# A recurrent block's gates computed gate by gate, and three output products that read their activations ahead, into the place of their low parts

## The chip, the cores and the metric

The kernel runs on one core of one Trainium2 chip, as one program. The metric is the device time of one execution in microseconds. The core has a matrix engine (TensorE, PE in the profile), a vector engine (VectorE, DVE), a scalar engine (ScalarE, ACT), a general engine (GpSimd, POOL) and a sync engine (SyncE, SP), which here only issues DMAs. Each engine works through its own instructions in order and waits on semaphores for the others.

## What is computed

One inference step of a model of two layers on 512 prompt rows and 8 x 16 sample rows (640 tokens, five tiles of 128). The first layer is recurrent, the second is stick-breaking attention with 16 heads. Between the two, the residual stream is normed and projected to shared keys and values. What the change touches, cut from the reference:

```python
def rg_lru(x, h0, w_r, b_r, w_i, b_i, lam):
    r = jax.nn.sigmoid(block_diag(x, w_r, b_r))
    i = jax.nn.sigmoid(block_diag(x, w_i, b_i))
    log_a = -LRU_C * r * jax.nn.softplus(-lam)
    a = jnp.exp(log_a)
    u = jnp.sqrt(-jnp.expm1(2.0 * log_a)) * (i * x)
    ...                                   # h = a * h + u along time

def recurrent_mixer(hn, ...):
    xb, zg = jnp.split(hn @ w_in, 2, axis=-1)
    xb, conv_new = causal_conv(xb, conv0, conv_w, conv_b)
    y, hT = rg_lru(xb, h0, ...)
    return (y * jax.nn.silu(zg)) @ w_out, hT, conv_new

x = x + gate * rms_norm(out, g_post[l])   # after each layer
```

The model's width D is 2048, the recurrent width 4096. Everything is fp32.

## The kernel before

**Precision.** A product of two fp32 operands is made of three matmuls of rounded operands: high by high, high by low, low by high (`mm3`, lines 101 to 103). A high part is a copy on ACT that rounds (`wh` line 87, `yh` line 777), the low part is the difference on DVE (`wl` line 88, `yl` line 778). Every weight and every activation tile that comes from memory therefore passes through ACT and then DVE before PE can use it. The split weights have three places (`WB`), their raw form four (`RB`, tag `wr`).

**The recurrent stage** (`recurrent`) goes through 16 blocks of 256 recurrent features, two halves of 128. For a block, `silu_gates` and `conv` make two products with the input weight `w_in` (`pair_product`): a scheme with seven instead of eight block products, over four accumulators in PSUM called `pc`, `pa`, `pb`, `pd`. The seven units have the names S1, X11, S4, S2, X12, S3, X22; each is 21 matmuls of 128x320. Two plain products with `xv` stand between S4 and S2. `keep` (line 561) copies an accumulator to SBUF on ACT so that its bank can be used again: `pa` holds X11, then S2, then S3, and each of these has to be copied before the next begins. The weights are split some steps ahead by a generator that `ahead` moves on, at a high priority (`urgent`).

`lru` computes the two gates r and i of the block: for each half and each gate two column halves, each a group of six matmuls in one of four banks (`psg`), and a sigmoid on ACT (line 702). Then come, in a fixed chain, Exp and Tanh on ACT (lines 712 and 716, with a table load), some operations on DVE, Sqrt (line 724, another table load), the scan along time, and the store of the block's y to DRAM (`yd`).

**The output products** (`out_product`) run three times: over the first 16 K tiles of the recurrent output, over the second 16, and over the attention's output (`yd` twice, then `od`). A product goes through chunks of one 512 column block and some token tiles; in its first chunk it also loads its 16 activation tiles, two ahead of their use, each into a raw tile `yr` that takes one of the four places of `wr`, and splits it into `yh` and `yl`. Those live in a ring of 8 tiles of four K tiles each (tag `h`), which the normed activations use too.

**Beside the second of them**, `mid` adds the residual to the finished token tiles: `residual` (line 851) reads x in four pieces a token tile into `xx`, two of which exist. The last head of the attention runs in one stretch with the beginning of the third product.

**What sets the order.** The instructions of an engine are put in order when the kernel is built, by a scheduler that follows the order of the program, readiness and priorities (`high_priority`). A tile's place is waited for by the first instruction that writes into it; a DMA that waits holds the queue of its issuing engine, SP for the weights, activations and x.

Of the kernel before, what the change touches and what calls it, by code (L numbers as in the profile page):

```python
# [11 lines left out]
F32 = mybir.dt.float32  # L12
# [36 lines left out]
class Trunk:  # L49
# [487 lines left out]
    def pair_product(self, ep, evac):  # L537


        nc = self.nc  # L540
        kw = dict(skip_group_check=True)

        def bank(n):
            return self.ring("quad", 4, n)[:, :HALF]

        def seven(ps, i, first):
            hi, lo = self.weights()
            c = slice(HALF * i, HALF * i + HALF)
            for n, x in enumerate(self.pairs):
                self.mm3(ps, hi[:, n, :], lo[:, n, :], x[:, 0, c], x[:, 1, c], first and n == 0, n == NP - 1, **kw)  # L550
            self.ahead()

        def plain(ps, w, half, first):
            c = slice(HALF * half, HALF * half + HALF)
            for n, k in enumerate(PLAIN):
                mh, ml = self.hT[k]
                self.mm3(ps, w[0][:, n, :], w[1][:, n, :], mh[:, c], ml[:, c], first and n == 0, k == KD - 1, **kw)

        def keep(ps, tag="keep", bufs=2):
            t = ep.tile([P, HALF], F32, tag=tag, name=tag, bufs=bufs)  # L560
            nc.scalar.activation(t, ps, AF.Copy)
# [24 lines left out]
        evac(1, 1, a, p5, ALU.add)  # L586
        seven(d, X22, False)
        evac(0, 1, d, u3, ALU.subtract)
# [94 lines left out]
    def lru(self, j, ep, block, zs):  # L683
        nc = self.nc
        V, A, G = nc.vector, nc.scalar, nc.gpsimd
        pv2, st, xf, xh, xl = block
        gw = [self.weights() for _ in range(2)]
        gate_bank = lambda n: self.half(n, "psg2") if n < 2 else self.bank("psg2")
        rs, qs = [], []
        for h in range(2):  # L690
            pv = pv2[:, h, :]
            fs = slice(P * h, P * h + P)
            g = []
            for i in range(2):
                hi, lo = gw[i]
                v = ep.tile([P, T], F32, tag="gq"[i], name="gq"[i], bufs=2)
                for c in range(2):
                    ps = gate_bank((2 * i + c) % 4)[:, :HALF]
                    s = slice(HALF * c, HALF * c + HALF)
                    for k in range(2):  # L700
                        self.mm3(ps, hi[:, k, fs], lo[:, k, fs], xh[k][:, s], xl[k][:, s], k == 0, k == 1)
                    last = A.activation(v[:, s], ps, AF.Sigmoid, bias=pv[:, 5 + i : 6 + i])
                g.append(v)
            rs.append(g[0])
            V.tensor_tensor(xf[h], g[1], xf[h], ALU.mult)
        self.ahead()


        for h in range(2):
            q = ep.tile([P, T], F32, tag="q", name="q", bufs=2)  # L710
            with self.tc.issue_after(last.ins):
                last = A.activation(q, rs[h], AF.Exp, scale=self.nk8[:, 2 * j + h : 2 * j + h + 1])
            qs.append(q)
        for h in range(2):
            with self.tc.issue_after(last.ins):
                last = A.activation(rs[h], rs[h], AF.Tanh, scale=self.k4[:, 2 * j + h : 2 * j + h + 1])
        for r, q in zip(rs, qs):
            e = ep.tile([P, self.HW + 1], F32, tag="tmp", name="e", bufs=self.TMP)[:, :T]
            V.tensor_scalar_add(q, q, 1.0)
            V.scalar_tensor_tensor(e, r, 1.0, q, op0=ALU.add, op1=ALU.mult)  # L720
            V.scalar_tensor_tensor(q, e, -4.0, q, op0=ALU.add, op1=ALU.mult)
        for r in rs:
            with self.tc.issue_after(last.ins):
                A.activation(r, r, AF.Sqrt, scale=0.25)
        for h, (r, q) in enumerate(zip(rs, qs)):
            f = 2 * j + h
            pv = pv2[:, h, :]
            V.scalar_tensor_tensor(r, r, -1.0, q, op0=ALU.mult, op1=ALU.mult)
# [12 lines left out]
        G.dma_start(self.O["state"][:, 2 * j : 2 * j + 2, :], st)  # L741
# [19 lines left out]
    def out_product(self, src, w, chunks, evac, fill=iter(())):  # L761


        nc = self.nc
        ys, slots = [], []

        def load(k):
            nonlocal slots
            if k % 4 == 0:
                slots = [self.hp.tile([P, 4, T], F32R, tag="h", name=n) for n in ("yh", "yl")]  # L770
            yh, yl = (x[:, k % 4, :] for x in slots)
            if k in self.local:
                raw = self.local[k]
            else:
                raw = self.wp.tile([P, self.WW], F32, tag="wr", name="yr", bufs=self.RB)[:, :T]
                nc.sync.dma_start(raw, src[P * k : P * k + P, :])
            self.last_split = nc.scalar.activation(yh, raw, AF.Copy).ins  # L777
            nc.vector.tensor_tensor(yl, raw, yh.bitcast(F32), ALU.subtract)  # L778
            ys.append((yh, yl))

        for c, (toks, n) in enumerate(chunks):
            cs = slice(512 * n, 512 * n + 512)
            ps = {t: self.acc("acc") for t in toks}

            def mm(k, t, hi, lo):
                ts = slice(P * t, P * t + P)
                yh, yl = ys[k]
                self.mm3(ps[t], yh[:, ts], yl[:, ts], hi, lo, k == 0, k == 15)

            last = c + 1 == len(chunks)  # L790
            early = 10 if last else 16
            for k in range(0, early, 2):
                hi, lo = self.wsplit(w[n, :, k : k + 2, :], 512)
                if len(ys) < 16:
                    load(k)
                    load(k + 1)
                for kk in range(2):
                    for t in toks:
                        mm(k + kk, t, hi[:, kk, :], lo[:, kk, :])
                if c > 0:  # L800
                    next(fill, 0)
# [84 lines left out]
    def attention_begin(self):  # L886
# [8 lines left out]
        return self.out_product(self.od, self.I["w_out_b"], chunks, gate)  # L895

    def attention_out(self, product):
        nc, O = self.nc, self.O
# [10 lines left out]
    def mid(self, oacc, ss, ss1, bp):  # L909
# [566 lines left out]
```

## Time and profile before

| | us |
|---|---|
| median of 3 runs | 2911.41 (2906.17 to 2912.74) |
| profiled execution | 2916.01 |
| its span | 2914.3 |
| recurrent stage | to about 1040 |
| product of the first 16 K tiles | 1046 to 1268 |
| product of the second 16, with the residual | to about 1550 |
| shared keys and values, heads, third product | to the end |

Times in the profile are microseconds from the span's start. A row of the timeline has the start, the duration, the engine, the line, the operation, output and inputs by their names in the program, shapes, a count, and in brackets the idle time before it with what ended it. Matmuls are pipelined: one lasts longer than the distance to the next, and that distance is the pace. In a window of PE, the columns are its length, busy time and matmuls, the granted clock of TensorE as a share of full speed, the DMA engines' mean share and their rate. A row of the view of waits gives who waited, for whom, the sum, how many times and the longest.

### The profile page before, as it was taken

How to read it: one execution, taken by the hardware profiler on the slowest of the kernel's cores; microseconds unless marked ns; L12 is line 12 of the kernel's file. 1: busy time of each engine (PE TensorE's matmuls, PEld its weight loads, DVE VectorE, ACT ScalarE, POOL GpSimd, SP SyncE). 2: the span in 40 equal slices, each digit the busy share in tenths (PEclk: the TensorE clock that was granted, in tenths of full speed). 3: DMA queues.
4: the chain of work that ended last, by engine and by line, in shares of the span. 5: the costliest groups of instructions: out<-in, count | busy, mean ns of one | idle time of the engine just before them, and what ended most of it. 6: DMA issues, size and time to landing. Idle time of an engine off the chain costs nothing.

```text
span 2914.3 us, 48223 instructions
## 1 busy us (share of the span) xinstructions
PE 2837.1 (97%) x18784; PEld 2520.8 (86%) x18784; DVE 1977.9 (68%) x2867; ACT 1607.8 (55%) x2464; POOL 420.3 (14%) x589
## 2 busy tenths in 40 slices
PE   6899999999999999999999999999999999999998
PEld 4799999999999977778788999778989999897886
DVE  7677776777677766634568877777666766667335
ACT  5466555655565566533456666674455555546323
POOL 0011222222222200001113322001000000001000
PEclk9899999999999999999999999999999999999999
DMA  9866676667666666555567666663565555656636
GB/s 338 303 143 150 162 163 152 146 164 160 158 146 162 143 195 190 167 147 163 186 209 254 226 209 214 203 200 115 185 197 168 182 175 183 198 169 197 208 109 224
DMA packets 246003, 536.49 MB, mean 184 GB/s; under 512 B 22520, under 2 KB 106616, under 8 KB 244624
## 3 DMA queue, kind: packets, MB, share of 16 engines
q1 hardware_dynamic: 219056, 442.01, 47.7%
q0 software_dynamic: 26720, 91.42, 15.5%
q8 instruction: 147, 2.41, 0.3%
q14 instruction: 80, 0.66, 0.1%
HBM read 496.24 MB, written 37.11 MB: 183 GB/s over the span
## 4 chain that ended last, share of the span: by engine, by line
PE 79%; ACT 6%; DVE 4%; DMA 2%; issue 2%; POOL 0%; DVEq 0%; POOLq 0%; SPq 0%; ACTq 0%
PE acc L101 7%; PE acc L102 7%; PE acc L103 7%; PE psh L101 6%; PE acck L101 5%; PE psh L103 5%; PE psh L102 5%; PE acck L103 5%; PE acck L102 5%; PE pa L101 3%; PE pa L103 3%; PE pa L102 3%; PE psa L198 2%; DVE wl L88 1%; PE pc L101 1%
## 5 line engine op out<-in xcount | busy, mean ns | idle before, releaser
L88 DVE TENSOR_TENSOR wl<-wr,wh 128x1024 fp32r<-128x1024 f32 x216 | 270.3, 1252 | 289.4 <-ACT wh L87 288.1
L87 ACT ACTIVATE wh<-wr 128x1024 fp32r<-128x1024 f32 x216 | 228.2, 1056 | 382.1 <-PE acc L103 228.6
L101 PE MATMUL acc<-wh,yh 128*128 128x512 f32 x960 | 378.8, 395 | 10.3 <-ACT yh L777 5.6
L102 PE MATMUL acc<-wl,yh 128*128 128x512 f32 x960 | 378.3, 395 | 7.7 <-DVE wl L88 7.7
L103 PE MATMUL acc<-wh,yl 128*128 128x512 f32 x960 | 377.0, 394 | 0.3 <-DVE yl L778 0.3
L186 DVE TENSOR_TENSOR wa<-wa,wa 128x1024 bf16<-128x1024 f32 (+1 forms) x256 | 308.6, 1240 | 24.9 <-ACT wa L185 22.7
L101 PE MATMUL psh<-nh,wh 128*128 128x320 f32 x1024 | 323.9, 316 | 0.0
L103 PE MATMUL psh<-nh,wl 128*128 128x320 f32 x1024 | 318.9, 311 | 0.0
L102 PE MATMUL psh<-nl,wh 128*128 128x320 f32 x1024 | 317.4, 310 | 0.0
L185 ACT ACTIVATE wa<-wa 128x1024 bf16<-128x1024 f32 x256 | 263.1, 1052 | 67.2 <-DVE wa L186 46.7
L101 PEld LDWEIGHTS acc<-wh,yh 128*128 128x128 f32 x960 | 182.1, 190 | 58.4 <-issue 8.7
L102 PEld LDWEIGHTS acc<-wl,yh 128*128 128x128 f32 x960 | 182.5, 190 | 47.7 <-DVE wl L88 10.3
L103 PEld LDWEIGHTS acc<-wh,yl 128*128 128x128 f32 x960 | 182.2, 190 | 39.9 <-DVE yl L778 2.2
L101 PEld LDWEIGHTS psh<-nh,wh 128*128 128x128 f32 x1024 | 192.3, 188 | 19.3 <-DVE ql L1112 12.6
L101 PE MATMUL pa<-xs,wh 128*128 128x320 f32 x630 | 194.8, 309 | 0.0
L103 PE MATMUL pa<-xs,wl 128*128 128x320 f32 x630 | 194.7, 309 | 0.0
L102 PE MATMUL pa<-xs,wh 128*128 128x320 f32 x630 | 194.7, 309 | 0.0
L103 PEld LDWEIGHTS psh<-nh,wl 128*128 128x128 f32 x1024 | 192.4, 188 | 0.5 <-DVE wl L88 0.2
L102 PEld LDWEIGHTS psh<-nl,wh 128*128 128x128 f32 x1024 | 192.4, 188 | 0.1
L101 PE MATMUL acck<-nh,wh 128*128 128x320 f32 x512 | 161.5, 315 | 0.0
L481 POOL DMA_DIRECT2D sum<-w_in_a_dram x90 | 79.4, 882 | 559.3 <-DVE wl L88 262.9
L103 PE MATMUL acck<-nh,wl 128*128 128x320 f32 x512 | 158.3, 309 | 0.0
(354 smaller groups left out, 7312.4 us busy)
## 6 DMA issues: line engine op xcount, KB each, us to landing
wa<-w_ada_dram SPq DMA_DIRECT2D x192, 512.0 KB, 4.7
wr<-w_out_a_dram SPq DMA_DIRECT2D x96, 512.0 KB, 4.1
sum<-w_in_a_dram POOLq DMA_DIRECT2D x90, 448.0 KB, 5.6
wr<-w_in_b_dram SPq DMA_DIRECT2D x64, 512.0 KB, 5.3
ck<-cache_k_dram SPq DMA_DIRECT2D x64, 512.0 KB, 6.7
cv<-cache_v_dram SPq DMA_DIRECT2D x64, 512.0 KB, 5.3
wr<-w_out_b_dram SPq DMA_DIRECT2D x56, 512.0 KB, 4.2
raw<-w_in_a_dram SPq DMA_DIRECT2D x60, 448.0 KB, 4.2
```

The costliest lines, as they stand in the source:

```text
L87: nc.scalar.activation(hi[:, :n], raw, AF.Copy)
L88: nc.vector.tensor_tensor(lo[:, :n], raw, hi[:, :n].bitcast(F32), ALU.subtract)
L101: mm(out, sh, mh, start=start, stop=False, **kw)
L102: mm(out, sh, ml, start=False, stop=False, **kw)
L103: mm(out, sl, mh, start=False, stop=stop, **kw)
L185: nc.scalar.activation(parts[i], raw, AF.Copy)
L186: nc.vector.tensor_tensor(parts[2] if i else raw, raw, parts[i], ALU.subtract)
L198: nc.tensor.matmul(ps[32 * j : 32 * j + 32, :], self.c3[:, 4 * g + j, :], ws[j // 2][i][:, j % 2, :], start=g + i == 0, stop=g == 3 and i ...
L481: self.nc.gpsimd.dma_start(self.big[tag], self.quarter(w, i), accum_op=ALU.add)
```

## The change

There are four edits. `keep` gets the high priority that the weights' splits have. `lru` computes the first gate for both halves, then the second gate for both, and moves the weights on after each gate. `out_product` reads an activation tile straight into the place of its low part, which DVE then overwrites; it reads groups of four K tiles, the first group before its first chunk, each next group when it begins to split the one before; the splits of the first four have a high priority. The last head's output, which never leaves the core, is named by `kept`. `mid` has six places for `xx` instead of two.

```diff
         def keep(ps, tag="keep", bufs=2):
             t = ep.tile([P, HALF], F32, tag=tag, name=tag, bufs=bufs)
-            nc.scalar.activation(t, ps, AF.Copy)
+            with self.tc.high_priority(200):
+                nc.scalar.activation(t, ps, AF.Copy)
             return t
...
-        for h in range(2):
-            pv = pv2[:, h, :]
-            fs = slice(P * h, P * h + P)
-            g = []
-            for i in range(2):
-                hi, lo = gw[i]
+        for i in range(2):
+            hi, lo = gw[i]
+            for h in range(2):
...
-                    ps = gate_bank((2 * i + c) % 4)[:, :HALF]
+                    ps = gate_bank(2 * h + c)[:, :HALF]
...
-        self.ahead()
+            self.ahead(1 - i)
...
+        def fetch(k):
+            hi, lo = (self.hp.tile([P, 4, T], F32R, tag="h", name=n) for n in ("yh", "yl"))
+            for kk in range(k, k + 4):
+                yh, yl = hi[:, kk - k, :], lo[:, kk - k, :]
+                if kk not in kept:
+                    nc.sync.dma_start(yl.bitcast(F32), src[P * kk : P * kk + P, :])
+                raws.append((yh, yl))
         def load(k):
-            if k in self.local:
-                raw = self.local[k]
-            else:
-                raw = self.wp.tile([P, self.WW], F32, tag="wr", name="yr", bufs=self.RB)[:, :T]
-                nc.sync.dma_start(raw, src[P * k : P * k + P, :])
-            self.last_split = nc.scalar.activation(yh, raw, AF.Copy).ins
-            nc.vector.tensor_tensor(yl, raw, yh.bitcast(F32), ALU.subtract)
+            if k % 4 == 0 and len(raws) < 16:
+                fetch(len(raws))
+            yh, yl = raws[k]
+            raw = self.local[k] if k in kept else yl.bitcast(F32)
+            with self.tc.high_priority(200 if k < 4 else 0):
+                self.last_split = nc.scalar.activation(yh, raw, AF.Copy).ins
+                nc.vector.tensor_tensor(yl, raw, yh.bitcast(F32), ALU.subtract)
             ys.append((yh, yl))
+        fetch(0)
...
-            ch = self.residual(t, oacc, ss, self.I["x"][ts, :], bp, 2)
+            ch = self.residual(t, oacc, ss, self.I["x"][ts, :], bp, 6)
```

**ACT in a recurrent block.** From Exp (`q<-g`) to the third copy of an accumulator, before:

```order
L712 ACTIVATE q<-g,nk_100 128x640
L716 ACTIVATE g<-g,k_99 128x640 x2
L561 ACTIVATE keep_3691<-pc_3663 128x320
L87 ACTIVATE wh<-sum_3182 128x896
L724 ACT_TABLE_LOAD
L724 ACTIVATE g<-g 128x640 x2
L87 ACTIVATE wh<-raw 128x896
L730 ACTIVATE q<-q,mone 128x640
L87 ACTIVATE wh<-rest 128x896
L730 ACTIVATE q<-q,mone 128x640
L561 ACTIVATE keep<-pa_3664 128x320
```

and with the change, the same stretch:

```order
L714 ACTIVATE q<-g,nk_100 128x640
L718 ACTIVATE g<-g,k_99 128x640 x2
L87 ACTIVATE wh<-sum_3182 128x896
L562 ACTIVATE keep<-pa_3664 128x320
L726 ACT_TABLE_LOAD
L726 ACTIVATE g<-g 128x640
L87 ACTIVATE wh<-raw 128x896
L726 ACTIVATE g<-g 128x640
L87 ACTIVATE wh<-rest 128x896
L732 ACTIVATE q<-q,mone 128x640
```

The copy of `pa` has moved from behind the table load, the Sqrts and two splits to ahead of them, and one Sqrt has fallen behind the split of `raw`.

**PE in the same block.** The last plain product (`pd` with `xv`) and what follows it, with buffer numbers, before:

```order
L102 MATMUL pd7_3749<-xv_1429,wh_3686 128x320
L103 MATMUL pd7_3749<-xv_1429,wl_3687 128x320
L101 MATMUL pb7_3748<-xs_261,wh_3742 128x320
L102 MATMUL pb7_3748<-xs_261,wh_3742 128x320
L103 MATMUL pb7_3748<-xs_261,wl_3743 128x320
```

and with the change:

```order
L102 MATMUL pd7_3749<-xv_1429,wh_3686 128x320
L103 MATMUL pd7_3749<-xv_1429,wl_3687 128x320
L101 MATMUL pa7_3664<-xs_261,wh_3714 128x320
L102 MATMUL pa7_3664<-xs_261,wh_3714 128x320
L103 MATMUL pa7_3664<-xs_261,wl_3715 128x320
```

The 21 matmuls of S2 (`pa` with the weight `wh_3714`) now come ahead of X12 (`pb` with `wh_3742`, the split of `raw`); before, X12 began first and S2 came after its first groups.

**ACT at the end of the recurrent stage**, from a sigmoid of the last block on; `yh` belongs to the first output product and `wh<-wr` is its first weight. Before:

```order
L702 ACTIVATE g<-psg_11239,pv 128x320
L87 ACTIVATE wh<-wr 128x1024
L702 ACTIVATE q<-psg_11248,pv 128x320
L702 ACTIVATE q<-psg_11256,pv 128x320
L712 ACT_TABLE_LOAD
L712 ACTIVATE q<-g,nk_100 128x640 x2
L716 ACTIVATE g<-g,k_99 128x640 x2
L777 ACTIVATE yh<-yr 128x640
```

and with the change:

```order
L702 ACTIVATE q<-psg_11238,pv 128x320
L784 ACTIVATE yh<-yl 128x640 x4
L702 ACTIVATE q<-psg_11248,pv 128x320
L702 ACTIVATE q<-psg_11256,pv 128x320
L714 ACT_TABLE_LOAD
L714 ACTIVATE q<-g,nk_100 128x640 x2
L718 ACTIVATE g<-g,k_99 128x640 x2
L87 ACTIVATE wh<-wr 128x1024
```

Four `yh` have moved ahead of the last two sigmoids, and the weight's split from ahead of them to behind Tanh (`g<-g,k`).

More of the change, by code (lines that the diff above doesn't have):

```diff
@@ L688, in lru @@
         gate_bank = lambda n: self.half(n, "psg2") if n < 2 else self.bank("psg2")
-        rs, qs = [], []
-        for h in range(2):
-            pv = pv2[:, h, :]
-            fs = slice(P * h, P * h + P)
-            g = []
-            for i in range(2):
-                hi, lo = gw[i]
+        gates, qs = [], []
+        for i in range(2):
+            hi, lo = gw[i]
+            for h in range(2):
+                pv = pv2[:, h, :]
+                fs = slice(P * h, P * h + P)
                 v = ep.tile([P, T], F32, tag="gq"[i], name="gq"[i], bufs=2)
                 for c in range(2):
-                    ps = gate_bank((2 * i + c) % 4)[:, :HALF]
+                    ps = gate_bank(2 * h + c)[:, :HALF]
                     s = slice(HALF * c, HALF * c + HALF)
@@ L702, in lru @@
                     last = A.activation(v[:, s], ps, AF.Sigmoid, bias=pv[:, 5 + i : 6 + i])
-                g.append(v)
-            rs.append(g[0])
-            V.tensor_tensor(xf[h], g[1], xf[h], ALU.mult)
-        self.ahead()
+                if i:
+                    V.tensor_tensor(xf[h], v, xf[h], ALU.mult)
+                else:
+                    gates.append(v)
+            self.ahead(1 - i)
+        rs = gates
         for h in range(2):
@@ L759, in accumulators, with out_product @@
         return [bp.tile([P, D], F32, tag=f"oacc{t}", name=f"oacc{t}") for t in range(TT)]
-    def out_product(self, src, w, chunks, evac, fill=iter(())):
+    def out_product(self, src, w, chunks, evac, fill=iter(()), kept=()):
         nc = self.nc
-        ys, slots = [], []
-        def load(k):
[L768 to L771, printed above, removed]
-            if k in self.local:
-                raw = self.local[k]
-            else:
-                raw = self.wp.tile([P, self.WW], F32, tag="wr", name="yr", bufs=self.RB)[:, :T]
-                nc.sync.dma_start(raw, src[P * k : P * k + P, :])
-            self.last_split = nc.scalar.activation(yh, raw, AF.Copy).ins
-            nc.vector.tensor_tensor(yl, raw, yh.bitcast(F32), ALU.subtract)
+        ys, raws = [], []
+        def fetch(k):
[5 more added lines that the diff above has]
+                raws.append((yh, yl))
+        def load(k):
+            if k % 4 == 0 and len(raws) < 16:
[5 more added lines that the diff above has]
+                nc.vector.tensor_tensor(yl, raw, yh.bitcast(F32), ALU.subtract)
             ys.append((yh, yl))
+        fetch(0)
         for c, (toks, n) in enumerate(chunks):
@@ L893, in gate @@
             self.nc.vector.tensor_tensor(self.oacc[t][:, 512 * n : 512 * n + 512], ps, self.gmap(t, n), ALU.mult)
-        return self.out_product(self.od, self.I["w_out_b"], chunks, gate)
+        return self.out_product(self.od, self.I["w_out_b"], chunks, gate, kept=(NHEAD - 1,))
     def attention_out(self, product):
```

## The prediction

> **What bounds the kernel now.** The page's first part comes first, then TensorE's waits.
>
> ```profile
> PE 2837.1 (97%) x18784; PEld 2520.8 (86%) x18784; DVE 1977.9 (68%) x2867; ACT 1607.8 (55%) x2464; POOL 420.3 (14%) x589
> ```
>
> PE works for 97% of the span, and the change removes no matmul. All it can win is PE's waits (77 us in all) and what follows them. The view of waits says where they are:
>
> ```profile
> PE pb L103 <- DVE wl L88: 12.3, 15, 0.9
> PE acc L102 <- DVE wl L88: 7.7, 4, 3.1
> PE acc L101 <- ACT yh L777: 5.6, 1, 5.6
> PE acc L101 <- ACT wh L87: 4.8, 2, 4.5
> ```
>
> The first is a small stall that comes back in 15 blocks of the recurrent loop; the others are single long stalls in the output products (`acc`). A long stall costs more than its idle time, which the windows of PE show (busy time, matmuls, granted clock, DMA share, GB/s):
>
> ```profile
> 1040.00:1052.00 12.00, 6.43 (x19) 0.73 0.19 55
> 1268.00:1280.00 12.00, 6.97 (x24) 0.86 0.47 149
> 1440.00:1450.00 10.00, 9.23 (x41) 1.00 0.99 374
> 1450.00:1460.00 10.00, 7.69 (x21) 0.66 0.86 290
> 1460.00:1470.00 10.00, 10.00 (x45) 1.00 0.87 295
> 2676.00:2686.00 10.00, 7.78 (x22) 0.66 0.63 190
> ```
>
> The row from 1460 is PE undisturbed: 45 matmuls in 10 us, 0.222 us each. Every other window falls short, and four have a granted clock under 1: after a long wait PE runs slowly for a while. What a place loses is its missing matmuls times 0.222 us. I call the places J1 (1040, loop to first product), J2 (1268, first half of the product to the second), J3 (1440 to 1460, residual beside the second half) and J4 (2676, last head beside the attention's product).
>
> **The recurrent loop.** One period on PE, ACT and DVE:
>
> ```profile
> 346.38 0.31 PE L101 MATMUL pb<-xs,wh 128*128 128x320 f32 x1
> 346.52 0.31 PE L102 MATMUL pb<-xs,wh 128*128 128x320 f32 x1
> 347.69 0.42 PE L103 MATMUL pb<-xs,wl 128*128 128x320 f32 x1 [0.86 <-DVE wl L88]
> 342.68 1.28 ACT L724 ACT_TABLE_LOAD   x1
> 345.25 0.94 ACT L87 ACTIVATE wh<-raw 128x896 fp32r<-128x896 f32 x1
> 348.38 0.41 ACT L561 ACTIVATE keep<-pa 128x320 f32<-128x320 f32 x1
> 345.08 1.55 DVE L728 SCALAR_TENSOR_TENSOR g<-g,q 128x640 f32<-128x640 f32 x2
> 346.55 1.08 DVE L88 TENSOR_TENSOR wl<-raw,wh 128x896 fp32r<-128x896 f32 x1
> ```
>
> PE has issued two of `pb`'s matmuls, 0.15 us apart, which is this form's pace; the third needs the weight's low part, which DVE starts at 346.55 behind two gate operations. It starts 1.17 us after the second, so 1.02 us is lost. Fifteen times that is 15.3 us. PE comes to `pb` so early because `keep`, which frees the bank of `pa`, stands at 348.38 on ACT, behind the table load and three more operations. With `keep` ahead of them, PE puts the 21 matmuls of `pa`'s second unit (21 x 0.15 = 3.1 us) in front of `pb`. ACT splits that weight one gate operation earlier too. The gates themselves, now first one gate for both halves and then the other, cost nothing: the eight sigmoids take 8 x 0.47 = 3.8 us (row 1040.44 below has two in 0.94) beside 48 matmuls of 0.15 us, 7.2 us, and a bank comes round after four groups as before. Were that cover gone, PE would wait for a sigmoid, 0.47 us a block, 7.5 us in 16. The first gate's weight frees its buffer after 24 of the 48 matmuls instead of 36, so the next split can go earlier. A cover of 3.1 us more against a shortage of 1.02 us leaves 2 us. What is late next is a bank of the gates, whose reuse distance stays at four. I take the stall as gone in the steady periods and keep 0.8 us for the first two blocks, where weights arrive close to their use: **-14.5 us**, ends 0 and -15.3.
>
> **J1.** The rows of ACT, and what PE waited for:
>
> ```profile
> 1039.49 1.05 ACT L87 ACTIVATE wh<-wr 128x1024 fp32r<-128x1024 f32 x1
> 1040.44 0.94 ACT L702 ACTIVATE q<-psg,pv 128x320 f32<-128x320 f32 x2
> 1041.39 1.28 ACT L712 ACT_TABLE_LOAD   x1
> 1042.69 1.55 ACT L712 ACTIVATE q<-g,nk 128x640 f32<-128x640 f32 x2
> 1044.14 1.53 ACT L716 ACTIVATE g<-g,k 128x640 f32<-128x640 f32 x2
> 1045.58 0.72 ACT L777 ACTIVATE yh<-yr 128x640 fp32r<-128x640 f32 x1
> 1046.35 0.79 PE L101 MATMUL acc<-wh,yh 128*128 128x512 f32 x1 [5.57 <-ACT yh L777]
> ```
>
> Before, `wh` is split in good time and one `yh` stands behind the gate's chain. Now four `yh` stand ahead of the last two sigmoids and `wh` stands behind the chain. From 1039.49: four times 0.65 (start to start, rows 1271.80 and 1272.45 below) = 2.6, sigmoids 0.95, table 1.30, `q` 1.45, `g` 1.44, `wh` 1.05: 1048.3 instead of 1046.35. **+2 us**; ends 0 (the loads land before 1039) and +4 (each of the four waits half a microsecond for its load). The slow clock comes either way. The window has 19 matmuls, so it stays the dearest.
>
> **J2.**
>
> ```profile
> 1262.66 0.74 ACT L777 ACTIVATE yh<-yr 128x640 fp32r<-128x640 f32 x1 [8.88 <-DMA yr<-yd]
> 1267.11 0.74 ACT L777 ACTIVATE yh<-yr 128x640 fp32r<-128x640 f32 x1 [2.76 <-DMA yr<-yd]
> 1271.80 0.74 ACT L777 ACTIVATE yh<-yr 128x640 fp32r<-128x640 f32 x1 [3.96 <-DMA yr<-yd]
> 1272.45 1.04 ACT L87 ACTIVATE wh<-wr 128x1024 fp32r<-128x1024 f32 x1
> 1273.54 0.76 PE L101 MATMUL acc<-wh,yh 128*128 128x512 f32 x2 [4.53 <-ACT wh L87]
> 1255.07 0.33 SPq L776 DMA_DIRECT2D yr<-yd  x1
> yr<-yd SPq DMA_DIRECT2D x1, 320.0 KB, 7.6
> ```
>
> ACT stands at loads of the second half's y while `wh` of the first half's last weights wait behind them. One such load was issued at 1255.07, when the raw buffers that y shares with the weights gave it a place, and took 7.6 us. Now the loads go into the place of `yl`. The first half's last chunk has 240 matmuls (16 K tiles, five token tiles, three each); PE's wait comes 164 in, and the first four K tiles are passed after 60. Those 104 matmuls x 0.222 = 23 us, so the first loads go out at about 1245.5 instead of 1255. At 7.6 us they land by 1253, at twice that by 1261. ACT's four `yh` and two `wh` (4 x 0.65 + 2 x 0.95 = 4.5) then end before 1268. The window has 24 of 54 matmuls: 30 x 0.222 = **-6.7 us**, ends 0 and -6.7.
>
> **J3.**
>
> ```profile
> 1448.42 0.75 DVE L851 SCALAR_TENSOR_TENSOR oacc<-oacc,ss,xx 128x512 f32<-128x512 f32 x1 [2.37 <-DMA xx<-x_dram]
> 1450.37 0.75 DVE L851 SCALAR_TENSOR_TENSOR oacc<-oacc,ss,xx 128x512 f32<-128x512 f32 x1 [1.20 <-DMA xx<-x_dram]
> 1451.04 1.22 DVE L88 TENSOR_TENSOR wl<-wr,wh 128x1024 fp32r<-128x1024 f32 x1
> 1452.31 0.79 PE L102 MATMUL acc<-wl,yh 128*128 128x512 f32 x1 [3.09 <-DVE wl L88]
> ```
>
> DVE waits for tiles of x, of which two are in flight, with the weights' low parts behind it. Six tiles are issued ahead now, so the first six additions find theirs. The windows 1440 and 1450 miss 4 + 24 = 28 of 90 matmuls, 6.2 us. Beside them the remaining tokens' additions, after 1515, I leave at nothing: they have the same two lines of work and no long wait of PE. The same bytes pass in the same time, at a DMA share of 0.99: if bandwidth alone sets it, nothing is won. The nearest row speaks for the gain: at 0.87 and 295 GB/s (1460) PE keeps its pace. **-6 us**, ends 0 and -6.2.
>
> **J4.**
>
> ```profile
> 2678.22 1.22 PE L102 MATMUL acc<-wl,yh 128*128 128x512 f32 x2 [2.74 <-DVE wl L88]
> 2666.62 4.15 DVE L1126 RECIPROCAL ez<-ez 128x640 f32<-128x640 f32 x1
> 2676.97 1.20 DVE L88 TENSOR_TENSOR wl<-wr,wh 128x1024 fp32r<-128x1024 f32 x1
> ```
>
> DVE works without a gap from the reciprocal to `wl`. The loads come earlier now, but four `yh` on ACT (2.6 us) and one `wl` on DVE (1.2 us) stand ahead of the last head's chain, and low parts of y between its links. If all of it shows, PE idles 2.74 + 2.6 + 1.2 = 6.5 us, in pieces: for the scores, for `yl`, for `wl`, for the softmax. In the window 2676 the present stall costs 23 x 0.222 = 5.1 us, 2.74 idle and 2.4 of slow clock. With no slow clock 6.5 stands against 5.1, so +1.4; with it 8.9, so +3.8; none of it shows where `acc` of the other chunks fills in, so -3 at the best. I take **+2 us**, near the price without a slow clock since no piece is as long as 2.74; ends -3 and +4.
>
> The trace has the slow clock after a wait of 2.74 us. The Trainium skill, "TensorE: Matmul & The Clock Gate", section "HAM oscillation — how this bites in real kernels", puts the limit at idle gaps of about 3.4 us; the trace disagrees, since 2.74 sufficed. By that rule J4's pieces would all stay at full clock, and the sum would be 0.6 us lower.
>
> **Sum.** -14.5 + 2 - 6.7 - 6 + 2 = -23.2 us on the profiled execution, 2916.0 (span 2914.3): 2892.8. That execution lies 4.6 us over the median of the runs, 2911.4, so the forecast is **2888 us**.
>
> **Rivals.**
> - *The loop's stall only moves.* For it: DVE and ACT issue as much as before, and a bank or a weight may be late 3 us further on. Against: 3.1 us of cover for 1.02. Then only the junctions count: 2911.4 - 8.7 = 2903. Chance 0.10.
> - *The loads come no earlier than before*, because the places of `yl` free too late or the maps of the gate hold the DMA rings: J2 and J3 stay, 2911.4 - 14.5 + 4 = 2901. For it: 7.6 us for one load. Chance 0.08.
> - *Slower: weights queue behind the loads.* SP issues in order; a group of four waits for its place, and the weights' loads behind it wait too. Each late group then costs about J2's price, 6.7 us. There are 12 groups; from four on (4 x 6.7 = 27) the gain is used up, with eight it is 2888 + 54 = 2942. For it: ACT stood 8.88 us behind such a load. Against: PE frees the places in the order of the loads. Chance 0.05.
> - *All edits at their good ends*: -15.3 + 0 - 6.7 - 6.2 - 3 = -31.2: 2880. Chance 0.10. My forecast as it stands: 0.67.
>
> **The numbers.** A measurement here can tell 0.2% (5.8 us) from no change. The two milder rivals lie at 0.3 and 0.4% under the median, each with half of its chance on either side of 2905.6, hence faster 0.87, same 0.07, slower 0.06. The range goes from 2879 (the good ends) to 2903 (the rivals), with 0.85 in it.
>
> **What would show it.** Right: no wait of `pb` on `wl` in the loop and blocks 1 us shorter; at J1 a wait of about 7.6 us; no idle at J2; 88 or more matmuls in the 20 us of J3; several waits of 1 to 2 us at J4. Wrong: a new wait on a gate's bank or on `wl` in every block; PE waits at J2 for `wl` or ACT for `yl`; DVE still waiting for x.

## The result, and the profile after

The changed kernel takes 2894.27 us (median of 5 runs, 2893.11 to 2898.03), the kernel before 2911.41 (5 runs, 2906.17 to 2915.04). The ratio is 0.9946, with a 95% interval from 0.9931 to 0.9961: faster by 11 to 20 us. The forecast was 2888, the range 2879 to 2903. The profiled execution took 2893.11 us, its span is 2891.4.

The page's first part and TensorE's waits, the longest single ones, of the changed kernel:

```profile
PE 2824.8 (98%) x18784; PEld 2513.4 (87%) x18784; DVE 1969.2 (68%) x2867; ACT 1608.5 (56%) x2464; POOL 411.2 (14%) x589
```

```profile
PE acc L101 <- ACT wh L87: 7.4, 1, 7.4
PE zc L1221 <- DVE e L1158: 2.8, 1, 2.8
PE acc L102 <- DVE sr L282: 2.8, 1, 2.8
PE pa L101 <- ACT keep L562: 2.7, 3, 1.2
PE pas L1241 <- ACT e L1159: 2.6, 1, 2.6
PE acc L103 <- DVE yl L785: 1.5, 1, 1.5
```

The wait of `pb` for `wl`, 12.3 us in 15 pieces, is gone. What is left in the loop are three waits for `keep`. The other five lines lie at J1 (7.4), J3 (2.8 for `sr`) and J4 (2.8, 2.6 and 1.5). The windows of PE (length, busy time, matmuls, granted clock, DMA share, GB/s) at the same places, which all come earlier now; the first row is a stretch of the loop:

```profile
500.00:600.00 100.00, 100.00 (x678) 1.00 0.70 160
1023.00:1035.00 12.00, 5.46 (x13) 0.57 0.80 298
1250.00:1262.00 12.00, 12.00 (x54) 1.00 0.54 208
1420.00:1430.00 10.00, 7.21 (x32) 1.00 1.02 391
2650.00:2660.00 10.00, 8.08 (x31) 0.71 0.41 145
2660.00:2670.00 10.00, 7.33 (x57) 0.66 0.36 107
```

The loop runs without a gap. J1 has 13 matmuls of the 54 or 55 that fit, J2 all of them, J3 misses 13 of 45 in its window, and J4 is spread over two windows at a lowered clock.

To see where the time went, I cut every profile at four events on PE: the first and the last matmul of the gates, the first matmul of line 198 (it stands behind J1 in the first product), and the first of the shared keys (`acck`). The columns are the distances: loop, J1's part, the part with J2 and J3, and the rest with J4. All are microseconds; "median" is that of the timed runs.

| kernel | loop | J1 | J2, J3 | J4, rest | median |
|---|---|---|---|---|---|
| before | 865.4 | 70.2 | 408.4 | 1395.2 | 2911.41 |
| changed | 852.2 | 71.7 | 398.4 | 1399.6 | 2894.27 |
| `keep` alone | 850.7 | 70.4 | 408.7 | 1393.9 | 2893.83 |
| gates alone | 928.7 | 70.1 | 406.7 | 1396.6 | 2972.06 |
| products' reading alone | 866.7 | 71.5 | 401.3 | 1398.4 | 2909.76 |
| six tiles of x alone | 865.2 | 70.1 | 405.1 | 1394.8 | 2907.38 |
| changed, third product without priority | 852.2 | 71.5 | 398.4 | 1393.5 | 2888.50 |
| changed, third product as before | 852.2 | 71.0 | 398.1 | 1394.7 | 2889.98 |
| changed, first weights ahead | 852.5 | 63.6 | 399.3 | 1395.7 | 2886.62 |
| changed, stores of the stream late | 852.1 | 72.3 | 397.9 | 1399.3 | 2894.75 |
| changed, both (weights ahead, no priority) | 852.7 | 63.1 | 398.6 | 1392.8 | 2878.79 |
| changed, gates as before | 850.7 | 72.3 | 397.9 | 1400.5 | 2893.30 |
| changed, twelve tiles of x | 852.1 | 72.3 | 396.6 | 1397.9 | 2893.45 |
| both, gates as before | 851.4 | 63.2 | 400.5 | 1392.7 | 2882.17 |

A part that an edit does not touch repeats within 3 us (the last part is 1393.9 to 1396.6 in the kernel before and in the three single edits that leave the third product alone). From before to changed the parts give -13.2, +1.5, -10.0 and +4.4: -17.3 us. What comes ahead of the first gate is not in them. It ended at 175.1 us in the profile of before and between 169.0 and 174.5 in the others, two of which (the products' reading alone, x alone) have no edit in the recurrent stage: it waits for DMAs and differs from execution to execution. So the two profiles' difference, 22.9 us, holds 5.6 us that belong to no edit.

### The profile page after: what moved, and what is told of

Its sections match the earlier page's. It is cut to its first block, busy times and chain, and to the rows that moved or that the text cites. A ratio compares the mean times of both kernels' runs of the same rounds, so it can differ in the third digit from the quotient of the medians.

```text
span 2891.4 us, 48123 instructions
## 1 busy us (share of the span) xinstructions
PE 2824.8 (98%) x18784; PEld 2513.4 (87%) x18784; DVE 1969.2 (68%) x2867; ACT 1608.5 (56%) x2464; POOL 411.2 (14%) x589
## 4 chain that ended last, share of the span: by engine, by line
PE 88%; DVE 2%; DMA 1%; ACT 1%; issue 1%; POOL 0%; SPq 0%; DVEq 0%; POOLq 0%; ACTq 0%
PE acc L101 7%; PE acc L103 7%; PE acc L102 7%; PE psh L101 6%; PE acck L101 5%; PE psh L103 5%; PE psh L102 5%; PE acck L102 5%; PE acck L103 5%; PE pa L101 3%; PE pa L103 3%; PE pa L102 3%; PE pc L103 2%; PE pc L101 2%; PE pc L102 2%; PE psa L198 2%
## 5 line engine op out<-in xcount | busy, mean ns | idle before, releaser
L186 DVE TENSOR_TENSOR wa<-wa,wa 128x1024 bf16<-128x1024 f32 (+1 forms) x256 | 308.4, 1240 | 23.2 <-ACT wa L185 21.4
L102 PE MATMUL acck<-nl,wh 128*128 128x320 f32 x512 | 158.3, 309 | 0.0
```

The lines of the kernel that those rows point to most:

```text
L102: mm(out, sh, ml, start=False, stop=False, **kw)
L186: nc.vector.tensor_tensor(parts[2] if i else raw, raw, parts[i], ALU.subtract)
```

## The experiments

**Each edit alone.** `keep` alone is this on the kernel before:

```diff
-            nc.scalar.activation(t, ps, AF.Copy)
+            with self.tc.high_priority(200):
+                nc.scalar.activation(t, ps, AF.Copy)
```

> Before plus the priority of keep alone. My theory (keep alone lets PE lay S2 ahead of X12, and that removes the loop's stall): no wait of pb on wl in the steady blocks, the loop 12 to 15 us shorter, J1 to J4 as before; 2896 to 2900. Rival (the earlier release of the gates' weights gives the cover): the stall stays in part, under 5 us gained; about 2907.

Measured: 2893.83 us (2892.31 to 2896.12), ratio 0.995 (0.9936 to 0.9965). The loop is 14.7 us shorter, the other parts are those of before. In the medians, one line gives the whole gain of the change. A stretch of the loop in the kernel before and in this one, in the view of PE's windows:

```profile
500.00:600.00 100.00, 98.29 (x663) 1.00 0.67 155
500.00:600.00 100.00, 100.00 (x679) 1.00 0.70 160
```

The gates alone are the edit in `lru`:

```diff
-        for h in range(2):
-            for i in range(2):
+        for i in range(2):
+            for h in range(2):
...
-                    ps = gate_bank((2 * i + c) % 4)[:, :HALF]
+                    ps = gate_bank(2 * h + c)[:, :HALF]
...
-        self.ahead()
+            self.ahead(1 - i)
```

> Before plus the gates' order alone. My theory: without the priority of keep it gains nothing, and it costs: in its order on PE X12 comes 21 matmuls (3.1 us) earlier in a block than before, while ACT's split of its weight moves by about 1 us, so the stall grows by about 2 us in 15 blocks: 2938 to 2945. Rival (the gates' order is what removes the stall): the stall is gone, 2896 to 2900. A third reading, that it changes nothing: 2911.

Measured: 2972.06 us (2966.08 to 2973.31), ratio 1.0212 (1.0195 to 1.0229). Slower by 63 us, twice what was expected. PE's waits in that kernel, then a block of its loop on PE and two rows of ACT, from the timeline (start, duration, engine, line, operation, output and inputs, idle time before):

```profile
PE pb L101 <- ACT wh L87: 29.3, 14, 2.2
PE pb L103 <- DVE wl L88: 13.0, 15, 1.1
```

```profile
589.99 0.31 PE L103 MATMUL psg<-xh,wl 128*128 128x320 f32 x1
597.47 0.31 PE L103 MATMUL pd<-xv,wl 128*128 128x320 f32 x1
599.95 0.42 PE L101 MATMUL pb<-xs,wh 128*128 128x320 f32 x1 [2.17 <-ACT wh L87]
601.55 0.63 PE L103 MATMUL pb<-xs,wl 128*128 128x320 f32 x1 [1.04 <-DVE wl L88]
...
602.25 0.47 PE L101 MATMUL pc<-xs,wh 128*128 128x320 f32 x1
...
607.58 0.39 PE L103 MATMUL pc<-xs,wl 128*128 128x320 f32 x1
598.97 0.93 ACT L87 ACTIVATE wh<-raw 128x896 fp32r<-128x896 f32 x1
601.26 0.42 ACT L561 ACTIVATE keep<-pc 128x320 f32<-128x320 f32 x1
```

And in a block of the kernel before, whose `pb` starts at 346.38:

```profile
335.19 0.31 PE L103 MATMUL psg<-xh,wl 128*128 128x320 f32 x1
341.41 0.42 ACT L561 ACTIVATE keep<-pc 128x320 f32<-128x320 f32 x1
```

The chain behind the last gate, up to the split of `raw`, is not longer: 598.97 less 589.99 is 9.0 us, against 345.25 less 335.19, 10.1, before. But PE comes to `pb` 7.6 us after its last gate (597.47 and one step of 0.15) where it came after 11.2. The cover that is missing is a unit of 21 matmuls (3.1 us): `pc` for the second time, whose bank `keep` has to free. Before, that copy stands on ACT ahead of the second table load (341.41); here it has fallen behind the whole chain (601.26), and the unit behind `pb` (602.25). The idle time is 42.3 us. The rest of the loss is the clock: from 601.55 to 607.58 PE makes 22 steps in 6.0 us instead of 22 x 0.147 = 3.2, 0.267 a step. The granted clock is at half for one such stretch in each of 14 blocks, 6.8 us long in eight of them and 3.4 in six, 75.1 us in all. PE is idle in 7.0 of these; the other 68.1 us lose (0.267 - 0.147) / 0.267 of their length, 31 us. 42.3 + 31 less the 12.3 us of idle time before is 61. Each wait loses some 0.16 us beyond its idle time (1.02 against 0.86 in the prediction's rows), and there are 14 more waits than before: 2 us. That makes 63, as the 63.3 in the table. My expectation had the idle time and left out the clock.

The products' reading alone is the edit of `out_product`, with `fetch`, `kept` and the priority of the first four splits:

```diff
+            if k % 4 == 0 and len(raws) < 16:
+                fetch(len(raws))
+            yh, yl = raws[k]
+            raw = self.local[k] if k in kept else yl.bitcast(F32)
+            with self.tc.high_priority(200 if k < 4 else 0):
...
+        fetch(0)
```

> Before plus the output products' loads alone. My theory: J1 +2, J2 -6.7 (no wait of PE around the end of the product's first half), J4 +2 to +5, the loop's stall as before; 2907 to 2912, that is no clear gain. Rival (the loads come no earlier): J2 stays, 2914 to 2918.

Measured: 2909.76 us (2904.58 to 2914.92, 10 runs), ratio 1.0003 (0.9994 to 1.0012). J2 and J3's part gains 7.1 us; the loop, J1 and the last part lose 1.3, 1.3 and 3.2. The edit nets nothing, as expected.

Six tiles of x alone:

```diff
-            ch = self.residual(t, oacc, ss, self.I["x"][ts, :], bp, 2)
+            ch = self.residual(t, oacc, ss, self.I["x"][ts, :], bp, 6)
```

> Before plus six places for x alone. My theory (places are what DVE waited for in J3): 3 to 6 us gained in J3, nothing elsewhere; 2905 to 2908. Rival (the DMA rate of the stretch sets it): within 2 us of before, 2909 to 2912, with DVE waiting for x as long as before.

Measured: 2907.38 us (2905.02 to 2913.07, 10 runs), ratio 1.0 (0.9991 to 1.001). The part with J3 is 3.3 us shorter; the times can't tell that from nothing.

**J4: the priority or the loads.** The last part lost 4.4 us, more than the forecast's upper end. Two kernels on the changed one: the priority left out for the third product, and the third product's loads and splits wholly as before.

```diff
-            with self.tc.high_priority(200 if k < 4 else 0):
+            with self.tc.high_priority(200 if k < 4 and not kept else 0):
```

> The changed kernel, with the high priority of the first four activation splits taken away in the third product alone. My theory (four yh of high priority stand on ACT ahead of the last head's softmax chain and delay it, which is J4's loss): the end falls back to what it was before, 3 to 4.4 us less than the changed kernel, 2890 to 2891.5. Rival (the loads ahead of time are the loss: ACT and DVE have splits earlier, whatever their priority): within 1.5 us of the changed kernel, 2893 to 2895.

Measured: 2888.50 us (2887.46 to 2891.81), ratio 0.9931 (0.9913 to 0.9948). The last part is 6.1 us shorter than in the changed kernel.

```diff
         def load(k):
+            if kept:
+                raw = self.wp.tile([P, self.WW], F32, tag="wr", name="yr", bufs=self.RB)[:, :T]
+                nc.sync.dma_start(raw, src[P * k : P * k + P, :])
...
-        fetch(0)
+        if not kept:
+            fetch(0)
```

> The changed kernel, with the third product loading its activations as before (two ahead, through the weights' raw buffers). Both theories of J4's loss (priority, loads ahead): 4 to 5 us less than the changed kernel, 2889 to 2891, with PE's wait at the first scores of the cached keys 0.4 us and at acc 2.74 again. If it stays at 2894, the loss comes from elsewhere, as from where the weights' loads stand.

Measured: 2889.98 us (2884.68 to 2893.13), ratio 0.9932 (0.9912 to 0.9952), the last part 4.9 us shorter. So the loads that come earlier cost nothing there that the times show; the priority does. ACT in the changed kernel, and PE:

```profile
2635.72 0.74 ACT L784 ACTIVATE yh<-yl 128x640 fp32r<-128x640 f32 x1 [0.75 <-DMA yl<-od]
2637.71 0.74 ACT L784 ACTIVATE yh<-yl 128x640 fp32r<-128x640 f32 x1 [1.25 <-DMA yl<-od]
2638.35 0.42 ACT L1127 ACTIVATE z<-psh 128x320 f32<-128x320 f32 x1
2638.67 1.05 ACT L87 ACTIVATE wh<-wr 128x1024 fp32r<-128x1024 f32 x1
2639.62 0.73 ACT L1132 ACTIVATE ez<-z 128x640 f32<-128x640 f32 x1
```

```profile
2636.40 0.31 PE L103 MATMUL psh<-nh,wl 128*128 128x320 f32 x1
2649.21 1.93 PE L1221 MATMUL zc<-ck,qs 128*32 128x512 f32 x8 [2.79 <-DVE e L1158]
2663.10 1.11 PE L1241 MATMUL pas<-ident,e 128*128 128x128 f32 x4 [2.57 <-ACT e L1159]
```

The scores are ready behind 2636.40, but ACT stands at a `yh` until its load lands, 1.25 us idle, and the head's chain (`z`, then `ez`) begins behind it: `ez` starts 3.2 us after the last matmul of the scores. PE then waits for the chain twice, 2.79 and 2.57 us. Without the priority:

```profile
2642.39 0.44 ACT L1127 ACTIVATE z<-psh 128x320 f32<-128x320 f32 x1 [0.39 <-PE psh L103]
2643.09 0.74 ACT L784 ACTIVATE yh<-yl 128x640 fp32r<-128x640 f32 x1 [0.27 <-DMA yl<-od]
2643.74 0.72 ACT L1132 ACTIVATE ez<-z 128x640 f32<-128x640 f32 x1
```

`z` waits for PE's scores and no longer for a load; the two waits of PE are 1.3 and 0.7 us in that kernel. The wait for `wl` that the kernel before had at `acc` is back with 2.7 us, so PE's waits in this stretch sum to 5.1 us against 7.6 in the changed kernel. The rest of the 6.1 us is the clock: over the last part the granted clock is at half for 3.4 us here, and for 13.7 us in the changed kernel (2648.9 to 2655.8 and 2662.6 to 2669.4).

**J1: the weight behind the gate chain.** On the changed kernel, the first weights' split of a product put ahead:

```diff
-                hi, lo = self.wsplit(w[n, :, k : k + 2, :], 512)
+                with self.tc.high_priority(200 if c == 0 and k < 4 else 0):
+                    hi, lo = self.wsplit(w[n, :, k : k + 2, :], 512)
```

> The changed kernel, with the splits of the first two weights of each product's first chunk at the high priority too. My theory (J1's wait is the first weight's split behind Exp and Tanh on ACT, and nothing else is late): the wait of 7.4 us at the first acc goes to under 1 us and the slow clock behind it with it, 8 to 10 us less than the changed kernel, 2884 to 2887. Rival (the wait only moves: the next weights or activations are late behind the same chain): 0 to 4 us less, 2890 to 2895.

Measured: 2886.62 us (2883.69 to 2889.44), ratio 0.9926 (0.9905 to 0.9946). First ACT in the changed kernel, then in this one:

```profile
1020.75 2.61 ACT L784 ACTIVATE yh<-yl 128x640 fp32r<-128x640 f32 x4
1023.26 0.93 ACT L702 ACTIVATE q<-psg,pv 128x320 f32<-128x320 f32 x2
...
1026.96 1.53 ACT L718 ACTIVATE g<-g,k 128x640 f32<-128x640 f32 x2
1028.40 1.04 ACT L87 ACTIVATE wh<-wr 128x1024 fp32r<-128x1024 f32 x1
```

```profile
1018.57 1.06 ACT L87 ACTIVATE wh<-wr 128x1024 fp32r<-128x1024 f32 x1
...
1022.34 3.07 ACT L784 ACTIVATE yh<-yl 128x640 fp32r<-128x640 f32 x4
```

The split that stood behind Tanh at 1028.40 now stands at 1018.57, the wait of 7.4 us is gone (1.2 us for a `yl` are left), and J1's part is 8.1 us shorter. The loads were there early enough; the order on ACT hid it. That it takes the edit of the products for this is not shown: the weights were not put ahead in a kernel that reads as before. (The edit puts the third product's first weights ahead too, and the last part is 3.9 us shorter here; how much of that is theirs was not taken apart.)

**J3: what holds the tiles of x.** VectorE in the changed kernel, and PE behind it:

```profile
1423.04 0.75 DVE L859 SCALAR_TENSOR_TENSOR oacc<-oacc,ss,xx 128x512 f32<-128x512 f32 x1 [4.09 <-DMA xx<-x_dram]
1423.71 1.22 DVE L88 TENSOR_TENSOR wl<-wr,wh 128x1024 fp32r<-128x1024 f32 x1
```

```profile
1424.98 0.50 PE L102 MATMUL acc<-wl,yh 128*128 128x512 f32 x1 [2.79 <-DVE sr L282]
```

The wait for x is not gone, it comes at a later tile, and the `wl` behind it on VectorE holds PE (the profile names `sr`, which ends a moment later). Two causes were possible: six places are still too few, or the rate (the DMA share is 1.02 in the window of 1420). In one kernel the stores of the finished residual, 1 MB a token tile, were put behind all of `mid`, to give the loads the DMA engines:

```diff
-            nc.gpsimd.dma_start(self.x1d[ts, :], oacc[t])
...
+        for t in range(TT):
+            nc.gpsimd.dma_start(self.x1d[P * t : P * t + P, :], oacc[t])
```

> The changed kernel, with the five stores of the residual rows (x1d) moved to the end of mid. Theory A (the DMA rate of the stretch J3 is used up, and the stores take it from x and the weights): DVE's wait of 4 us for x and PE's of 2.8 us go, 2.5 to 3 us less, 2891 to 2892. Theory B (x waits for places and for SP's queue, not for the rate): the waits stay, 2893 to 2895.

Measured: 2894.75 us (2893.04 to 2896.01), ratio 0.995 (0.9933 to 0.9967). VectorE's two waits for x there (0.62 and 4.09) became three (0.28, 2.77 and 1.48), and the time stayed. In another kernel x got twelve places:

```diff
-            ch = self.residual(t, oacc, ss, self.I["x"][ts, :], bp, 6)
+            ch = self.residual(t, oacc, ss, self.I["x"][ts, :], bp, 12)
```

> The changed kernel with x read in twelve tiles in place of six in the residual beside the second product's second half. If the 4.1 us that VectorE waits there for a tile of x come from too few places, so that its load starts late, the wait goes and with it TensorE's 2.8 us: 2891 to 2892 us. Rival: the rate of the transfers at that place is the bound (the share of the DMA engines is 0.97 to 1.04 there), so more places only move the same wait: 2894 us, as the changed kernel.

Measured: 2893.45 us (2890.58 to 2898.12), ratio 0.9952 (0.9936 to 0.9967). VectorE has no wait for x there any more, and of PE's waits at J3 one of any size is left:

```profile
1432.48 0.50 PE L102 MATMUL acc<-wl,yh 128*128 128x512 f32 x1 [0.77 <-DVE wl L88]
```

The issues of the loads fit this. With twelve places, all twelve tiles that VectorE uses in this stretch are asked for by 1224.8, long ahead. With six, six are asked for by 1217.1 and the seventh at 1407.0, when the first addition has freed a place, into a stretch whose DMA share goes up to 1.02. So the places were too few; the rate in the stretch matters only for loads that come this late. The part gains 1.8 us in the profile, which the medians can't tell from the changed kernel.

**Together.** The weights ahead in the first two products, and no priority in the third:

```diff
-            with self.tc.high_priority(200 if k < 4 else 0):
+            with self.tc.high_priority(200 if k < 4 and not kept else 0):
...
-                hi, lo = self.wsplit(w[n, :, k : k + 2, :], 512)
+                with self.tc.high_priority(200 if c == 0 and k < 4 and not kept else 0):
+                    hi, lo = self.wsplit(w[n, :, k : k + 2, :], 512)
```

> The changed kernel with two edits at once: the third product's splits without the high priority, and the first 128 rows of the first weight tile's split of the first two products with it. If the waits that the two edits take away, after the loop and in front of the third product, are separate places on TensorE's chain, the gains add: 5.8 + 7.7 = 13.5 us under the changed kernel, so about 2881 us (2878 to 2884). Rival: the weights' split, put ahead, makes the loads of the second product's activations or its evacuations late, so that only the larger of the two is kept: about 2886 us.

Measured: 2878.79 us (2877.55 to 2881.66), ratio 0.9897 (0.9884 to 0.9911): 30 us under before and the fastest of all. The gains add. (The expectation names the first 128 rows of one weight tile; the edit puts the first two splits ahead, as above.) J1's window in it:

```profile
1023.00:1035.00 12.00, 12.00 (x55) 1.00 1.04 403
```

Last, the gates' order in this company: the changed kernel, and the one just named, with the gates as before.

```diff
-        for i in range(2):
-            for h in range(2):
+        for h in range(2):
+            for i in range(2):
...
-            self.ahead(1 - i)
+        self.ahead()
```

> The changed kernel with the two gates in the order of before (gate by gate within a half of the rows, weights released once). Theory: beside the early copies of keep, the order of the gates is worth 0 to 1.5 us, since the loop took 852.2 us in the changed kernel and 850.7 us where only keep was put ahead; so 2892.8 to 2894.3 us, and the loop's short waits for keep in the first blocks get smaller. Rival: the earlier release of the first gate's weights, at half of the gates, is what brings the transposes' weights in time in the changed kernel, and without it the loop shows waits for the split weights again: 0.47 us a block or more, 2902 us and up.

Measured: 2893.30 us (2889.24 to 2894.54), ratio 0.9943 (0.9931 to 0.9956). The loop is 1.5 us shorter; the time is that of the changed kernel.

> The kernel of the two edits (first weights put ahead, third product without priority), with the gates in the order of before besides. If the order of the gates is worth 0 to 1.5 us in this company, 2879.3 to 2881 us, and the fastest of all. Rival: without the early release of the gates' weights the loop waits for split weights, and it is slower than the kernel of the two edits alone by 7 us or more, 2888 us and up.

Measured: 2882.17 us (2879.48 to 2884.51), ratio 0.9907 (0.9894 to 0.9921). Its interval overlaps that of the kernel with the changed gates; the 3.4 us between the medians are of the size by which the phase ahead of the loop differs (173.8 against 169.1 us in the two profiles). So the gates' order is worth nothing measurable once `keep` is ahead, and no wait in the loop comes back without it. The rival that it brings the weights in time is out.

## Why the prediction came out as it did

- **The loop (-14.5): right in its cause, 1.3 us too much.** It measured -13.2; `keep` alone gave -14.7. In the steady blocks no wait is left. In the first blocks three waits for `keep` remain, 2.7 us, where 0.8 was kept in the sum. The 1.5 us between the changed kernel and `keep` alone go with the gates' order, and no wait in the view names them. The timeline has most of it: in 13 blocks of the changed kernel three matmuls of `pc` stand between the sixth and the seventh group of the gates, and the step behind the first matmul of the seventh group takes 0.23 us instead of 0.15, 1.1 us in all. Why it does is open.
- **"The gates cost nothing": true only in company, and so by luck.** The prediction priced the loss of their cover at 7.5 us, a sigmoid a block. Alone they cost 63 us, and by another way: the copy of `pc` fell behind the chain as that of `pa` had, a unit went with it, and the clock fell in 14 blocks. `keep` ahead brings both copies in front of the second table load, and both units in front of `pb`: the two edits meet in the same line of ACT.
- **J1 (+2): right, +1.5.** The wait is 7.4 us, as forecast 7.6. The prediction took the weight behind the chain as given; it was worth 8 us to move it.
- **J2 (-6.7): right.** No idle in the window, 54 matmuls of 54. The products' reading alone gave -7.1 in that part, of which about 1.3 belong to J3, where the slow clock lasted 3.4 us instead of 6.8.
- **J3 (-6): mis-sized, -3, and by another way.** The step "the first six additions find theirs" held, since the first eight do; but the ninth waits 0.62 us and the eleventh 4.09. This is the sign of being wrong that the prediction named, DVE still waiting for x. The prediction counted the tiles at the start of a token tile and not the ones that follow while all six places are in use. PE's wait fell only from 3.09 to 2.79 us. The 3 us come from the clock, which was at half for 6.8 us behind that wait before (1451.6 to 1458.4) and is full in the changed kernel. How much of this six places can claim is open: the clock at J3 is full in the kernel with the gates alone too, which has two places, and whether a wait of this length brings the slow clock goes by where it falls (last section). Six places alone gave 3.3 us in the part, twelve on the changed kernel another 1.8; with two places and the products as before, the same part already lies between 406.7 and 408.7.
- **J4 (+2): mis-sized, +4.4, past its upper end.** The idle time came about as summed. PE waits 7.6 us in this stretch (2.8, 2.6, 1.5, 0.4 and 0.3) and waited 3.4 before: 4.2 more, where the sum had 3.8 more if all of it showed. The step that failed is "no slow clock, since no piece is as long as 2.74": the granted clock is 0.71 and 0.66 in J4's two windows, behind waits of 2.79 and 2.57 us, and at half for 13.7 us against 6.8 before. The length of a piece is not what decides (last section). The pieces were also summed as work on ACT and DVE alone (2.6 and 1.2 us). An instruction with priority whose data is not there yet stops its engine besides, here for 0.75 and 1.25 us, and the chain behind it waits as well.

The sum by terms, -23.2, against -17.3 by parts: J3 3 us, J4 2.4, the loop 1.3, less about 1 us at J1 and J2. That is the 6 us by which the forecast was too low. The four places, forecast at -8.7 together, measured -4.1 in the parts, and the medians show nothing of it beside `keep` alone. The forecast holds by its largest term. None of the rivals came: the stall didn't move, and the weights did not queue behind the loads.

## What to carry to other kernels

Find out which edit of a bundle gives the gain: here one line of priority gave all of it, and the edit of the products netted zero until two orders on ACT were put right. A high priority paid here for copies whose inputs were there; put on one that still waited for a load, it handed that wait to everything behind it. When a reorder seems free, look at what it was covering on the other engine, in microseconds between the last producer and the first consumer.

## What the hardware showed that was not expected

The length of a wait does not decide whether PE's clock falls. The first matmuls after three waits at J3, in the kernel with `keep` alone,

```profile
1431.98 0.80 PE L102 MATMUL acc<-wl,yh 128*128 128x512 f32 x1 [3.13 <-DVE wl L88]
```

in the one with the products' reading alone,

```profile
1443.15 0.50 PE L102 MATMUL acc<-wl,yh 128*128 128x512 f32 x1 [3.14 <-DVE wl L88]
...
1444.19 0.57 PE L103 MATMUL acc<-wh,yl 128*128 128x512 f32 x1
...
1447.55 0.45 PE L102 MATMUL acc<-wl,yh 128*128 128x512 f32 x1
```

and in the kernel of both edits with the gates as before:

```profile
1421.97 0.50 PE L102 MATMUL acc<-wl,yh 128*128 128x512 f32 x1 [3.00 <-DVE sr L282]
```

After 3.13 us PE is slow at once, for 6.1 us (to 1438.1). After 3.14 it is fast for 1 us, then slow for 3.4. After 3.00 it is not slow at all. The kernel with the gates alone gives the reason, since there the slow stretch comes back in 14 blocks. Its first and its last end:

```profile
225.31 0.37 PE L102 MATMUL pc<-xs,wh 128*128 128x320 f32 x1
...
1051.41 0.34 PE L103 MATMUL pc<-xs,wl 128*128 128x320 f32 x1
```

They are 826.1 us apart, 242 times 3.4136; the block shown above ends 382.3 us after the first, 112 times 3.4131. All 14 ends lie within 0.17 us of one grid with a step of 3.413 us, though the slow stretches begin 61 to 65 us apart. The slow stretch of the products alone, 1444.19 to 1447.55, is one step long. So the clock is set at the marks of a grid that runs on its own. The Trainium skill, "TensorE: Matmul & The Clock Gate", section "Part 1: The HAM clock gate (the "warmup" mystery)", says that the activity is watched in free-running windows of 3413 ns; the trace agrees, 3.413. Cut at this grid, whose place in each profile is known from its own slow stretches, the waits read so (the idle time is the length of a window of PE less its busy time):

| kernel, place | wait | idle in one window, and in the next | clock |
|---|---|---|---|
| before, J3 | 3.09 | 2.4, 0.7 | slow from the mark between, for two windows |
| `keep` alone, J3 | 3.13 | 2.4, 0.7 | slow from the mark between, for two windows |
| products alone, J3 | 3.14 | 0.8, 2.3 | slow from the mark behind the second, for one |
| `keep` alone, J2 | 4.95 | 1.9, 3.0 | full in the second, slow behind it |
| both, gates as before, J3 | 3.00 | 1.6, 1.4 | full |
| changed, J3 | 2.79 | 1.4, 1.4 | full |
| changed, third product without priority, J3 | 2.25 | 0.7, 1.6 | full |
| gates alone, block at 599.95 | 2.17 and 1.04 | 2.6, 0.65 | slow from the mark between, for two windows |
| gates alone, first of the 14 blocks | 1.03 and 0.57 | 1.6, 0 | slow from the mark behind, for one |

In the output products, 2.3 us of idle time in one window of 3.4 was enough and 1.9 was not; and where the next window began with 0.65 or 0.7 us of idle time, it was followed by another slow one. This is no fixed border in idle time: in the loop, 1.6 us were enough in that first block, whose longest wait is 1.03 us:

```profile
219.97 0.41 PE L101 MATMUL pb<-xs,wh 128*128 128x320 f32 x1 [1.03 <-ACT wh L87]
221.09 0.42 PE L103 MATMUL pb<-xs,wl 128*128 128x320 f32 x1 [0.57 <-DVE wl L88]
```

What exactly a window is weighed by stays open. Of a wait of about 3 us one can't say beforehand whether the slow clock follows. The prediction read the rule as one on the length of a gap, and took its row of 2.74 us at J4 as a threshold. There the mark at 2677.0 divides that wait, and the window before the mark has 1.9 us of idle time, with other short waits. The length was the wrong quantity.
